# Sums of w_down's rows formed one pair later, one silu queued behind a copy, seven places for weights in the second half of down

## The chip, the cores and the metric

The kernel runs on one core of a Trainium2 chip. The metric is the device time of one execution in microseconds (us); lower is better. A core has a tensor engine (PE, with its weight loads shown as PEld), a vector engine (DVE), a scalar engine (ACT), GpSimd (POOL), and an engine that only issues transfers (SP). ACT and POOL can issue transfers too. Each engine works through its own list of instructions in order.

## The reference, cut to what matters

One layer of an encoder trunk on 512 tokens with 1024 channels, in float32. After the mixers and the cross-attention comes the gated MLP, and the change lies wholly in it:

```
hf = _rms_norm(x, norm_ffn_pre[l])
u = _dwconv_causal(hf @ w_up[l], ffn_dw[l]) + ffn_dw_b[l]     # 1024 -> 2 x 2816, causal conv of width 3
u_g, u_v = jnp.split(u, 2, axis=-1)
yff = (jax.nn.silu(u_g) * u_v) @ w_down[l]                    # 2816 -> 1024
x = x + _rms_norm(yff, norm_ffn_post[l])
```

## The kernel before, in words

**Precision.** Every float32 operand of a product is split into a high part (a cast on ACT: L202 for w_up, L1673 for w_down) and a low part (a subtraction on DVE: L203, L1674). A product is three matmuls: high by high, high by low, low by high (L245 is the line of all of them).

**The up projection (`up_jobs`).** The 2816 gated channels are 22 blocks of 128. Block j has a gate half (i = 0) and a value half (i = 1), each with a weight block of 1024 x 128. `plain(j, i)` computes a half in the direct way, into one PSUM bank; `done` then evacuates it on ACT (L1697, into the tile c), adds the two taps of the convolution on DVE (L627), and, after the value half, takes the silu of the gate half on ACT (L1700) and multiplies the two on DVE into `ns.quart` (L1702). Blocks 0 to 4, the even ones up to 18, and 20 and 21 are plain. The eight odd blocks 5 to 19 use `seven`, a scheme with seven products in place of eight: sums of weight quarters are formed on POOL (L1752 to L1756), sums of the tokens were formed once (`token_sums`, L1663 and L1665, on POOL, then split by `token_split`, L1669 and L1670), and the job runs in five bodies a to e. `body_a` makes a product into the bank `z.r2`, copies it to SBUF on ACT (L1778), and makes a second product into `z.r1`; `body_b` then accumulates into `z.r2` (L1783), so it must wait until the copy has read it. Between the bodies of odd block j lie the two halves of the plain block j − 1.

**Sums of w_down's rows (`Sums`, `ns.sums`).** The down projection uses seven products too, and its weight sums depend on nothing but w_down. The rows are taken in 11 pairs of 128-row blocks. For each pair, `load` brings two tiles of 512 KB from w_down, `add` forms four sums in place (L575 to L578, on POOL in this stage), and `store` writes the two tiles to a buffer in DRAM. Pairs 0 to 3 (`EARLY` is 4) are done much earlier, between other work. Pairs 4 to 10 are done in the up projection; their tiles `wp` use the two places dw0 and dw1, and their loads and stores are issued by ACT. Pair 4's load is issued in the first jobs of the up projection, its sums on POOL beside the token sums; then, at each odd block, one pair is stored, the next loaded, and its sums formed at the block's end. `sums_step` ties each to an instruction of `done` on the same engine.

**The down projection (`down_jobs`).** Two halves (phases), each over the 11 pairs of rows, each pair in two jobs, so 22 + 22 weight tiles ("raws"). The transfers (L594, by SP) bring them into four places dw0 to dw3, in turn; `weights` for tile n asks for tiles up to n + 2. The first phase makes four of the seven products in eight PSUM banks, `middle` evacuates them, and the second phase makes the other three. Its last four pairs are held back and multiplied bank by bank in `ends`, followed by the norm and the output.

**What sets the order.** Instructions are traced in program order, but a scheduler reorders them at build time by a simulated time line: each engine gets, among the instructions ready in that simulation, the one that stands first in the program. On the chip the lists then run in that fixed order. `tc.issue_after(x)` ties what it encloses behind instruction x on the same engine's list, without a wait for x to finish. Tiles with the same tag share a place, and a new tile waits until the last reader of the old one is done. In this program the tag `tokh` holds the high parts of the token sums during the up projection, and then (`late_places`, `down_places`) the sums of activations of pairs 4 to 10 (`pairs`) during the first half of down.

Of the kernel before, what the change touches and what calls it, by code (L numbers as in the profile page):

```python
# [25 lines left out]
P = 128  # L26
# [60 lines left out]
def hybrid_layer(ctx: ExitStack, tc: tile.TileContext, a: dict, out: bass.AP):  # L87
# [1112 lines left out]
    def then(f):  # L1200

        return None, None, f
# [485 lines left out]
    def up_jobs():  # L1688
# [1 line left out]
        HALF = S // 2  # L1690
        first, second = slice(0, HALF), slice(HALF, S)

        def done(j, i, ps):
            if i == 0:
                st[j] = ns.fp.tile([P, 2, S], F32, tag="c", name="c", bufs=2)
            c, ch = st[j], i * NF + j
            st["first"] = A.activation(c[:, i], ps, AF.Identity, bias=pc("fb", ch), scale=pc("fdw2", ch)).ins  # L1697
            st["taps"] = taps(c[:, i], ps, lambda k: pc("fdw01", k * 44 + ch), 3).ins
            if i == 1:
                A.activation(c[:, 0], c[:, 0], AF.Silu)  # L1700
                x = ns.quart[j // 2][:, 2 * (j % 2):2 * (j % 2) + 2]
                V.tensor_tensor(x.rearrange("p a b -> p (a b)"), c[:, 0], c[:, 1], ALU.mult)  # L1702

        def block(j, i):
            return cols(w_up, i * DFF + j * P)
# [1 line left out]
        def sums_step(what, q, anchor):  # L1707
            if q < NF // 2:
                with tc.issue_after(st[anchor]):
                    getattr(ns.sums, what)(q)  # L1710

        def plain(j, i, then=None):
            def body(hi, lo):
                ps = bank()
                channel_major(ps, (hi, lo), ns.hf)
                done(j, i, ps)
                if then:
                    then()
            return *block(j, i), body

        for n in range(4):
            def body(hi, lo, n=n):
                j, i = divmod(n, 2)
                if n == 0:
                    bg.drain("n0")
                ps = bank(("mm", "sc")[n % 2])
                if n == 3:
                    channel_major(ps, (hi, lo), ns.hf, first, lambda: bg.drain("n1"))
                else:
                    (channel_major if n else by_pass)(ps, (hi, lo), ns.hf, first)  # L1730
                held.append((j, i, ps, (hi, lo)))
                if n == 3:
                    open_ffn()
                    ns.sums.tile, ns.sums.queue = lambda: dw_tile("wp", 2), A
                    ns.sums.load(EARLY)
                    token_sums()
                    for j, i, ps, w in held:
                        (channel_major if i or j else by_pass)(ps, w, ns.hf, second)
                        done(j, i, ps)
            yield *cols(w_up, n % 2 * DFF + n // 2 * P), body, V, same, HALF_SHIFT  # L1740

        def seven(j):

            z = SimpleNamespace()

            def load_a():
                z.g, z.v = [load_block(j, i) for i in range(2)]
                w = split_weights(z.g, [P, NK, P], shift=HALF_SHIFT)
                z.s = ns.fp.tile([P, D], F32, tag="z7", name="sums2")
                a11, a12, a21, a22 = (x[:, c] for x in (z.g, z.v) for c in (slice(0, S), slice(S, D)))  # L1750
                s1, s2 = z.s[:, :S], z.s[:, S:]
                G.tensor_tensor(s1, a21, a22, ALU.add)  # L1752
                G.tensor_tensor(s2, s1, a11, ALU.subtract)
                G.tensor_tensor(a21, a11, a21, ALU.subtract)
                z.t = ns.fp.tile([P, S], F32, tag="th", name="s4")
                G.tensor_tensor(z.t, a12, s2, ALU.subtract)  # L1756
                return w

            def load_block(j, i):
                raw = dw_tile("wq", 2, 2)  # L1760
                SP.dma_start(raw.rearrange("p (k c) -> p k c", k=NK), block(j, i)[0])
                return raw

            def product(ps, w, k0, x, start):
                for k in range(4):
                    mm3(ps, w[0][:, k0 + k], w[1][:, k0 + k], x[0](k), x[1](k), start and k == 0, k == 3, True)

            def part(k0, t):
                return [lambda k, h=h: h[:, k0 + k, (first, second)[t]] for h in ns.hf]

            def summed(i):
                return [lambda k, h=h: h[:, i, k] for h in ns.tok]

            def body_a(*w):
                z.r1, z.r2 = bank("sc"), bank("tr")
                z.m = ns.fp.tile([P, 2, HALF], F32, tag="mu", name="mu")
                product(z.r2[:, first], w, 0, part(0, 0), True)
                A.copy(z.m[:, 0], z.r2[:, first])  # L1778
                product(z.r1[:, first], w, 4, part(4, 0), True)
                V.tensor_tensor(z.r1[:, first], z.r1[:, first], z.m[:, 0], ALU.add)  # L1780

            def body_b(*w):
                product(z.r2[:, first], w, 4, summed(1), False)  # L1783
                A.copy(z.m[:, 1], z.r2[:, first])
                product(z.r1[:, second], w, 0, summed(0), True)
                A.copy(z.m[:, 0], z.r1[:, second])

            def body_c(*w):
                z.w = w
                product(z.r2[:, first], w, 0, summed(2), False)  # L1790
                V.tensor_tensor(z.r2[:, second], z.r2[:, first], z.m[:, 0], ALU.add)

            def body_d(*w):
                product(z.r1[:, second], w, 0, part(4, 1), False)
                V.tensor_tensor(z.r1[:, second], z.r1[:, second], z.m[:, 1], ALU.add)
                done(j, 0, z.r1)

            def end():
                product(z.r2[:, first], z.w, 4, summed(3), False)
                done(j, 1, z.r2)  # L1800

            return (load_a, body_a, (lambda: split_weights(z.s, [P, NK, P], shift=HALF_SHIFT), None, body_b),
                    (lambda: split_weights(z.v, [P, NK, P], shift=HALF_SHIFT), None, body_c),
                    (lambda: split_weights(z.t, [P, 4, P], shift=HALF_SHIFT), None, body_d), then(end))
# [4 lines left out]
        def early_places():  # L1809
            ns.pair_sums = []  # L1810
            down_places(f"qa{NF // 2 - 1}", 2)

        def splits(*which):
            return lambda: [token_split(i) for i in which]

        def add(q):
            if q < NF // 2:
                ns.sums.add(q, G)
# [2 lines left out]
        yield plain(2, 0, splits(1))  # L1821
        yield plain(2, 1, splits(0))
        yield plain(3, 0, splits(2))
        yield plain(3, 1, splits(3))
        yield then(lambda: (early_places(), add(EARLY)))

        for q, j in enumerate(pairs, EARLY):
            load_a, body_a, b, c, d, e = pairs[j]
            a = load_a, None, body_a
            tail = {}  # L1830

            def first_half(hi, lo, tail=tail):
                tail.update(ps=bank(), w=(hi, lo))
                for k in range(4):
                    mm3(tail["ps"], hi[:, k], lo[:, k], ns.hf[0][:, k], ns.hf[1][:, k], k == 0, False)

            def second_half(j, tail=tail):
                hi, lo = tail["w"]
                for k in range(4, NK):
                    mm3(tail["ps"], hi[:, k], lo[:, k], ns.hf[0][:, k], ns.hf[1][:, k], False, k == NK - 1)  # L1840
                done(j, 1, tail["ps"])

            yield a
            yield plain(j - 1, 0)
            yield then(lambda q=q: sums_step("store", q, "first"))
            yield b
            yield (*block(j - 1, 1), first_half)
            yield then(lambda q=q: sums_step("load", q + 1, "taps"))
            yield c
            if j in (9, 13):  # L1850
                yield then(sums_of((j - 9) // 4))
            if j == NF - 3:
                yield then(lambda: down_places("z7", 2))
            yield d
            yield then(lambda j=j, f=second_half: f(j - 1))
            if j == NF - 3:
                yield then(sums_of(2))
            yield e
            yield then(lambda q=q: add(q + 1))
# [11 lines left out]
    def down_jobs():  # L1871
# [4 lines left out]
        def load(n):  # L1876
            while len(raws) < min(n, 2 * len(order)):
                (phase, q), job = order[len(raws) // 2], len(raws) % 2
                raw = dw_tile("dw")
                load_parts(raw, ns.sums.parts(phase, job, q))  # L1880
                raws.append(raw)

# [30 lines left out]

        def weights(phase, q, job):
            n = 2 * (phase * pairs + q) + job
            load(n + 3)
            if n == 0:
                activations(0, 0)
            if job and n + 1 < 2 * len(order):
# [184 lines left out]
```

## Time and profile before

| | |
|---|---|
| median of 3 runs | 1042.18 us (1041.12 to 1042.36) |
| the profiled execution: time, span | 1040.78 us, 1039.0 us |
| granted PE clock, mean | 0.997 |
| busy: PE, DVE, ACT, POOL | 1024.6, 860.9, 533.5, 263.9 us |
| the up projection's token sums to its last block | about 696 to 925 us of the span |
| first and last load of down (L594) | 875.2, 1011.5 us |

A row of the time order reads: start in us, duration in us, engine, line, operation, output <- inputs, and in square brackets the idle time of the engine ahead of it with what ended it. SPq, ACTq and POOLq are the engines' sequencers, where transfers are issued. In a row of waits stand: the waiting instruction, what it waited for, us in total, how often, the longest.

### The profile page before, as it was taken

To read this page: it belongs to the slowest core of one execution; us is meant where nothing else is said; L and a number is where in the kernel's file an instruction comes from. 1 tells how busy PE (TensorE), PEld (TensorE's weight loads), DVE (VectorE), ACT (ScalarE), POOL (GpSimd) and SP (SyncE) were. 2 spreads that over 40 slices of the span, in tenths; PEclk is the share of its full clock that TensorE was granted. 3 is DMA by queue.
4 is the path that set the end of the run, shared out by engine and by line. 5 is a ranking of instruction groups with operands and counts; after the bars stand their busy time and mean duration, and the time that the engine had idled before them with its cause. 6 is when DMAs were issued, how large, how long until landed. Compare 5 with 4: busy or idle time off the path is not lost.

```text
span 1039.0 us, 15182 instructions
## 1 busy us (share of the span) xinstructions
PE 1024.6 (99%) x5477; PEld 883.9 (85%) x5477; DVE 860.9 (83%) x1323; ACT 533.5 (51%) x893; POOL 263.9 (25%) x270
## 2 busy tenths in 40 slices
PE   8999999999999999999999999999899999999996
PEld 7888888888888988888888889998799899888885
DVE  7999999787788667888687798778879897799786
ACT  5322222376565365766634566654455455466662
POOL 4001000100020214342000031149376556026102
PEclk9999999999999999999999999999999999999999
DMA  7954344844534245766458843153456566326662
GB/s 254 315 168 107 102 155 144 269 142 115 150 97 133 83 136 151 201 183 170 148 182 262 244 128 119 60 157 107 159 186 199 182 220 211 103 81 196 211 204 88
DMA packets 194128, 169.40 MB, mean 163 GB/s; under 512 B 25295, under 2 KB 165692, under 8 KB 194053
## 3 DMA queue, kind: packets, MB, share of 16 engines
q1 hardware_dynamic: 187315, 145.08, 46.9%
q10 hardware_dynamic: 4178, 14.82, 3.9%
q0 software_dynamic: 2560, 8.54, 2.7%
q8 instruction: 43, 0.70, 0.3%
q14 instruction: 32, 0.26, 0.1%
HBM read 142.18 MB, written 26.23 MB: 162 GB/s over the span
## 4 chain that ended last, share of the span: by engine, by line
PE 90%; DVE 5%; ACT 2%; issue 2%; DMA 1%; ACTq 0%; SPq 0%; POOL 0%; POOLq 0%; DVEq 0%
PE ps_mm L245 39%; PE ps_av L245 25%; PE ps_tr L245 14%; PE ps_sc L245 10%; PE ps_tr L251 1%; DVE wl L203 1%; DMA dw<-sums 1%; DMA e<-in_w_in 1%; DVE c L627 1%; PE ps_mm L463 1%; PE ps_av L463 1%; DVE tokl L1670 0%; ACT wh L202 0%; DVE qa L1702 0%; DVE n L1674 0%
## 5 line engine op out<-in xcount | busy, mean ns | idle before, releaser
L202 ACT CAST wh<-wr 128x1024 fp32r<-128x1024 f32 (+1 forms) x124 | 129.4, 1046 | 193.6 <-PE ps_mm L245 67.5
L203 DVE TENSOR_TENSOR wl<-wr,wh 128x1024 fp32r<-128x1024 f32 (+1 forms) x124 | 163.6, 1321 | 31.8 <-ACT wh L202 31.2
L245 PE MATMUL ps_mm<-hth,wh 128*128 128x512 f32 (+1 forms) x472 | 173.5, 376 | 0.1
L245 PE MATMUL ps_mm<-htl,wh 128*128 128x512 f32 (+1 forms) x472 | 173.5, 376 | 0.0
L245 PE MATMUL ps_mm<-hth,wl 128*128 128x512 f32 (+1 forms) x472 | 173.2, 375 | 0.0
L245 PEld LDWEIGHTS ps_mm<-hth,wl 128*128 128x128 f32 x472 | 87.0, 188 | 15.7
L245 PEld LDWEIGHTS ps_mm<-hth,wh 128*128 128x128 f32 x472 | 87.0, 188 | 15.6 <-ACT hth L164 0.3
L245 PEld LDWEIGHTS ps_mm<-htl,wh 128*128 128x128 f32 x472 | 87.0, 188 | 15.3
L245 PE MATMUL ps_av<-hth,wh 128*128 128x512 f32 (+1 forms) x264 | 97.9, 371 | 0.0
L245 PE MATMUL ps_av<-htl,wh 128*128 128x512 f32 (+1 forms) x264 | 97.9, 371 | 0.0
L245 PE MATMUL ps_av<-hth,wl 128*128 128x512 f32 (+1 forms) x264 | 97.6, 370 | 0.0
L700 DVE SCALAR_TENSOR_TENSOR y<-y,par,y 128x508 f32<-128x508 f32 (+29 forms) x120 | 82.4, 725 | 0.0
L245 PEld LDWEIGHTS ps_av<-htl,wh 128*128 128x128 f32 x264 | 49.7, 188 | 8.2
L245 PEld LDWEIGHTS ps_av<-hth,wl 128*128 128x128 f32 x264 | 49.8, 188 | 8.1
L245 PEld LDWEIGHTS ps_av<-hth,wh 128*128 128x128 f32 x264 | 49.8, 189 | 7.9
L1673 ACT CAST wh<-dw 128x1024 fp32r<-128x1024 f32 x32 | 33.7, 1052 | 21.8 <-PE ps_av L245 6.2
L1674 DVE TENSOR_TENSOR wl<-dw,wh 128x1024 fp32r<-128x1024 f32 x32 | 39.4, 1233 | 6.3 <-ACT wh L1673 6.2
L1910 POOL TENSOR_TENSOR qa<-qa 128x256 f32<-128x256 f32 x11 | 26.6, 2431 | 58.5 <-DVE wr L1674 34.5
L245 PE MATMUL ps_tr<-htl,wh 128*128 128x512 f32 (+1 forms) x112 | 40.6, 363 | 0.0
L245 PE MATMUL ps_tr<-hth,wh 128*128 128x512 f32 (+1 forms) x112 | 40.6, 363 | 0.0
L245 PE MATMUL ps_tr<-hth,wl 128*128 128x512 f32 (+1 forms) x112 | 40.4, 360 | 0.0
L1127 POOL TENSOR_SCALAR fbias<-ck,cq 128x128 f32<-128x128 f32 (+3 forms) x32 | 21.4, 673 | 66.9 <-DVE st L1133 61.8
(558 smaller groups left out, 2737.3 us busy)
## 6 DMA issues: line engine op xcount, KB each, us to landing
wr<-in_w_in SPq DMA_DIRECT2D x38, 512.0 KB
wr<-in_w_gate SPq DMA_DIRECT2D x32, 512.0 KB
wr<-in_w_up SPq DMA_DIRECT2D x28, 512.0 KB
dw<-sums SPq DMA_DIRECT2D x44, 256.0 KB
wr<-in_w_branch SPq DMA_DIRECT2D x16, 512.0 KB
wq<-in_w_up SPq DMA_DIRECT2D x16, 512.0 KB
wp<-in_w_down ACTq DMA_DIRECT2D x14, 512.0 KB
sums<-wp ACTq DMA_DIRECT2D x14, 512.0 KB
```

Source lines behind the costliest of these rows:

```text
L202: last_weights[:] = [order(A.copy(hi, raw[:, :n])).ins, low.tensor_tensor(lo, raw[:, :n], hi.bitcast(F32), ALU.subtract).ins]
L203: low.tensor_tensor(lo, raw[:, :n], hi.bitcast(F32), ALU.subtract).ins]
L245: steps_of[:] = [PE.matmul(ps, lhs, rhs, start=start, stop=stop, skip_group_check=again).ins]
L251: turns.append(PE.transpose(ps, x, ident[:n, :n]).ins)
L463: keep(PE.matmul(banks[c][:, :S // 2], w[p == 1][:, k, c * P:(c + 1) * P], ht[p == 2][:, i * 4 + k, :S // 2], start=(i, p, k) == (0, 0, 0) ...
L627: ins = V.scalar_tensor_tensor(dst[:, s:], src[:, :S - s], w(k), dst[:, s:], ALU.mult, ALU.add)
L700: ins = V.scalar_tensor_tensor(dst[:, s:], src[:, :S - s], pc("conv_dw", k * 4 + j), dst[:, s:], ALU.mult, ALU.add)
L1127: G.tensor_scalar(bias[:, :w], ck[j][:, :w], -1.0, cq[:, qt, head:head + 1], ALU.mult, ALU.add)
L1673: A.copy(hi, x)
L1674: return V.tensor_tensor(lo, x, hi.bitcast(F32), ALU.subtract).ins
L1910: G.tensor_tensor(z[:, 1], z[:, 2], z[:, 1], ALU.subtract)
```

## The change

Three edits, all in the MLP.

1. The sums of w_down's pairs 4 to 10 move one odd block later. The load of pair 4 is no longer issued in the first jobs of the up projection but during block 5, behind an instruction of `done`; its sums are formed at the end of block 5; the first store is in block 7, and the store of pair 10 in block 19, where there was none.
2. For block 3, `done` stops after the taps. Its silu and multiply (now `product_of`) are traced inside `body_a` of block 5, and on ACT the silu is tied behind that body's first copy (L1778).
3. In the second half of down, a tile of three weight places, `dw2`, is laid where `pairs` lay (tag `tokh`). Of each seven weight tiles the first three go there, the other four to dw0 to dw3, and the transfers are asked for six ahead instead of three, from the last job but one of the first half.

```
-        def done(j, i, ps):
+        def done(j, i, ps, ends=True):
...
-            if i == 1:
-                A.activation(c[:, 0], c[:, 0], AF.Silu)
-                x = ns.quart[j // 2][:, 2 * (j % 2):2 * (j % 2) + 2]
-                V.tensor_tensor(x.rearrange("p a b -> p (a b)"), c[:, 0], c[:, 1], ALU.mult)
+            if i == 1 and ends:
+                product_of(j)
+
+        def product_of(j):
+            c = st[j]
+            A.activation(c[:, 0], c[:, 0], AF.Silu)
+            x = ns.quart[j // 2][:, 2 * (j % 2):2 * (j % 2) + 2]
+            V.tensor_tensor(x.rearrange("p a b -> p (a b)"), c[:, 0], c[:, 1], ALU.mult)
...
                     ns.sums.tile, ns.sums.queue = lambda: dw_tile("wp", 2), A
-                    ns.sums.load(EARLY)
                     token_sums()
...
-                A.copy(z.m[:, 0], z.r2[:, first])
+                copied = A.copy(z.m[:, 0], z.r2[:, first]).ins
+                if j == 5:
+                    with tc.issue_after(copied):
+                        product_of(3)
...
-        yield plain(3, 1, splits(3))
-        yield then(lambda: (early_places(), add(EARLY)))
-
-        for q, j in enumerate(pairs, EARLY):
+        yield plain(3, 1, splits(3), False)
+        yield then(early_places)
+
+        for q, j in enumerate(pairs, EARLY - 1):
...
-            yield then(lambda q=q: sums_step("store", q, "first"))
+            if q >= EARLY:
+                yield then(lambda q=q: sums_step("store", q, "first"))
...
-            yield then(lambda q=q: sums_step("load", q + 1, "taps"))
+            yield then(lambda q=q: sums_step("load", q + 1, "first" if q < EARLY else "taps"))
...
-                raw = dw_tile("dw")
+                if phase and len(raws) == 2 * pairs:
+                    parts["more"] = ns.fp.tile([P, 3, D], F32, tag="tokh", name="dw2")
+                k = (len(raws) - 2 * pairs) % 7
+                raw = parts["more"][:, k] if phase and k < 3 else dw_tile("dw")
...
-            load(n + 3)
+            load(n + (3 if n < 2 * pairs - 2 else 6))
```

More of the change, by code (lines that the diff above doesn't have):

```diff
@@ L1710, in sums_step, with plain @@
                     getattr(ns.sums, what)(q)
-        def plain(j, i, then=None):
+        def plain(j, i, then=None, ends=True):
             def body(hi, lo):
@@ L1715, in body @@
                 channel_major(ps, (hi, lo), ns.hf)
-                done(j, i, ps)
+                done(j, i, ps, ends)
                 if then:
```

## The prediction

> **What bounds the kernel now.** First the page's line of busy times, then the waits of the tensor engine (PE) from 640 us to the end, where all edited code lies.
>
> ```profile
> PE 1024.6 (99%) x5477; PEld 883.9 (85%) x5477; DVE 860.9 (83%) x1323; ACT 533.5 (51%) x893; POOL 263.9 (25%) x270
> ```
>
> ```profile
> PE ps_tr L245 <- ACT mu L1778: 3.1, 1, 3.1
> PE ps_mm L245 <- ACT n L1673: 0.9, 1, 0.9
> PE ps_mm L245 <- DVE n L1674: 0.3, 1, 0.3
> ```
>
> PE sets the time. An edit that takes no matmul away (none here does) can give only idle PE time and slow PE time, and from 640 us on the rows leave three waits: one of 3.1 us near 744 us and two together 1.2 us near 1016 us. Next the time order around the first.
>
> ```profile
> 733.58 0.28 PE L245 MATMUL ps_tr<-hth,wl 128*128 128x256 f32 x1
> ...
> 740.35 0.39 PE L245 MATMUL ps_mm<-hth,wl 128*128 128x512 f32 x1
> 743.83 0.38 PE L245 MATMUL ps_tr<-tokh,wh 128*128 128x256 f32 x1 [3.08 <-ACT mu L1778]
> ```
>
> ```profile
> 733.01 0.78 ACT L1697 ACTIVATE c<-ps_mm,par 128x512 f32<-128x512 f32 x1
> 733.68 1.04 ACT L1669 CAST tokh<-qa 128x1024 fp32r<-128x1024 f32 x1
> 741.27 0.63 ACT L1700 ACTIVATE c<-c 128x512 f32<-128x512 f32 x1 [6.54 <-DVE c L627]
> ...
> 742.74 0.77 ACT L1697 ACTIVATE c<-ps_av,par 128x512 f32<-128x512 f32 x1
> 743.42 0.36 ACT L1778 COPY mu<-ps_tr 128x256 f32<-128x256 f32 x1
> ```
>
> The bank that the copy L1778 reads was filled by 733.86 (733.58 + 0.28). The scalar engine (ACT) ran the copy 9.6 us later. It had been idle 6.54 us in front of the silu of pair 3 (L1700), which waited for the vector engine (DVE), and the copy stood three places behind that silu. PE cannot start the product of L1783 into the bank before it is read.
>
> ```profile
> 717.40 2.77 DVE L203 TENSOR_TENSOR wl<-wr,wh 128x1024 fp32r<-128x1024 f32 x1
> ...
> 737.51 1.22 DVE L203 TENSOR_TENSOR wl<-sums,wh 128x1024 fp32r<-128x1024 f32 x1
> ...
> 740.43 0.74 DVE L627 SCALAR_TENSOR_TENSOR c<-ps_mm,par,c 128x511 f32<-128x511 f32 x1
> ```
>
> DVE reaches the tap that releases the silu only at 740.43 to 741.17. One split takes 2.77 us at 717 and 1.22 us at 737. What differs is GpSimd (POOL), which works without a pause up to 733 us:
>
> ```profile
> 711.47 1.31 POOL L575 TENSOR_TENSOR wp<-wp 128x512 f32<-128x512 f32 x1
> ...
> 719.04 2.28 POOL L576 TENSOR_TENSOR wp<-wp 128x512 f32<-128x512 f32 x1
> ...
> 726.32 2.28 POOL L577 TENSOR_TENSOR wp<-wp 128x512 f32<-128x512 f32 x1
> 728.55 2.41 POOL L1665 TENSOR_TENSOR qa<-qa 128x1024 f32<-128x1024 f32 x1
> 730.91 2.29 POOL L578 TENSOR_TENSOR wp<-wp 128x512 f32<-128x512 f32 x1
> ```
>
> Then the clock in stretches cut at the gap and, in a second answer of the same view, one later stage (columns: length, then busy time of PE, PEld, DVE, ACT, POOL, granted clock, DMA share, GB/s):
>
> ```profile
> 740.70:743.80 3.10, 0.04 (x1) 0.00 (x0) 1.41 (x2) 2.53 (x5) 0.00 (x0) 1.00 0.46 189
> 743.80:748.00 4.20, 4.17 (x25) 4.18 (x26) 4.20 (x8) 2.41 (x5) 0.00 (x0) 0.68 0.72 236
> 748.00:749.00 1.00, 1.00 (x5) 0.80 (x5) 0.96 (x3) 1.00 (x2) 0.00 (x0) 0.65 0.61 175
> ```
>
> ```profile
> 880.00:900.00 20.00, 20.00 (x125) 17.99 (x124) 13.98 (x19) 10.10 (x15) 0.05 (x1) 1.00 0.41 118
> ```
>
> Right behind the gap the granted clock is 0.68 and 0.65 for about 5 us. So the gap costs more than itself: 4.17 x (1 − 0.68) + 1.00 x (1 − 0.65) = 1.33 + 0.35 = 1.7 us. Last, from the chain of waits, what PE takes at full clock for a run of matmuls 256 wide (0.12 us each) and 512 wide (0.23 us each):
>
> ```profile
> 871.27 1.42 PE ps_tr L245 x12
> ...
> 979.84 1.36 PE ps_sc L245 x6
> ```
>
> **The change, part by part.**
>
> (1) The product of pair 3 goes behind the copy of block 5. Two instructions move, the silu (0.63 us) and one multiply; none is added. The copy is then free to run once ACT has done L1697 of 733.01 and L1669 of 733.68 (ends 734.72); with the other L1697 (0.77) ahead of it, it ends near 734.72 + 0.77 + 0.36 = 735.9. PE asks for it at 740.7. The 3.08 us wait goes, with a cover of 4.8 us, and with it, I take it, the slow clock: 3.1 + 1.7 = 4.8 us.
>
> What is late next? Behind the silu stands the cast of the weights for block 4's second half (in the row left out, between L1700 and L1697). If nothing else changed, the silu would run at 741.27, that cast would end near 742.9 and its low part on DVE near 744.1 (1.22 us more), whereas PE, after two products of 12 matmuls of 0.12 us, would ask at 740.7 + 2.8 = 743.5. That is a remainder of 0.6 us, bounded by 0 and 0.6, unless DVE comes earlier, which part 2 does.
>
> (2) The sums start one pair later. Removed at 711 to 733: four POOL instructions, 1.31 + 2.28 + 2.28 + 2.29 = 8.16 us, and two loads of 512 KB on ACT's queue ahead of them. The token sum of 728.55 then ends near 731.0 − 5.9 = 725.1, and a DVE split meets POOL for 8.16 us less. By the two split rows DVE gets back at most 8.16 x (1 − 1.22/2.77) = 4.6 us, and nothing if its queue there was held by other inputs. I take 2.5 us, since the taps, which read PSUM, took 0.74 us in this stretch. On the sum it is worth only the 0.6 us above, already counted.
>
> The first load now goes out behind block 4's L1697, with no transfer ahead of it on its places; its POOL sums have until the next pair's POOL work is done. The pairs between keep their pattern with the number one lower. What is new lies at the other end, in the stage of block 19: four POOL sums and two stores.
>
> ```profile
> 871.46 0.33 ACTq L582 DMA_DIRECT2D sums<-wp  x1
> ...
> 893.17 0.78 ACT L1697 ACTIVATE c<-ps_mm,par 128x512 f32<-128x512 f32 x1
> ```
>
> ```profile
> 875.18 0.34 SPq L594 DMA_DIRECT2D dw<-in_w_down  x1
> ...
> 882.11 2.18 SPq L185 DMA_DIRECT2D wr<-in_w_up  x2
> ...
> 897.88 6.68 SPq L185 DMA_DIRECT2D wr<-in_w_up  x2
> ```
>
> The sums cost DVE at most the same 4.6 us there. From 880 to 900 us DVE is idle 20 − 13.98 = 6.0 us, which hides it. The last stores move from 871.46 to behind the L1697 at 893.17. Before, the first load of down into those places came 875.18 − 871.46 = 3.7 us behind the first store. Now it is due near 897, past the first two weight loads of the up projection (882.11) and beside the last two (897.88). On SP's queue, which is in order, those could be held a microsecond; they serve blocks 20 and 21, which are asked for only at the end of the up projection. I cost this at nothing; without that cover it is 1 us.
>
> (3) Seven places in the second half of down. No instruction is added; 10 of 22 loads get another address and all are issued six ahead instead of three. The place (the old pair sums) falls free when the last activation of the first half is split, about when the first such load could go anyway.
>
> ```profile
> 1011.48 0.32 SPq L594 DMA_DIRECT2D dw<-sums  x1
> ```
>
> ```profile
> 1013.51 1.05 ACT L1673 CAST dw<-dw 128x1024 fp32r<-128x1024 f32 x1 [1.10 <-DMA dw<-in_w_down]
> 1014.91 1.14 ACT L1673 CAST n<-dw 128x512 fp32r<-128x512 f32 x2 [0.35 <-DMA dw<-sums]
> ```
>
> ```profile
> ACT n L1673 <- DMA dw<-sums: 6.2, 5, 2.0
> ```
>
> ```profile
> 1016.10 0.50 PE L245 MATMUL ps_mm<-n,htl 128*128 128x512 f32 x1 [0.91 <-ACT n L1673]
> 1016.91 0.73 PE L245 MATMUL ps_mm<-n,htl 128*128 128x512 f32 x2 [0.31 <-DVE n L1674]
> ```
>
> The last load goes out at 1011.48 because a place was not free, and lands for the casts at 1014.91, which release PE. Three loads earlier is 1.5 pairs of PE work, so this chain starts some microseconds sooner than the 1.2 us that PE lacks. Bounds 0 and 1.2 us; I take 1.2, as ACT's casts of this kind waited 6.2 us for transfers and for little else. No slow clock follows here.
>
> [...]
>
> The sum: 3.1 + 1.7 + 1.2 = 6.0 us off the profiled execution, span 1039.0 to 1033.0, time 1040.8 to 1034.8 (1.8 us lie around the span). The median of the runs, 1042.18, is 1.4 us above that execution, so it goes to **1036.2**.
>
> **The rivals.**
>
> A. The tail stays. The last chain is bound by DVE and ACT work itself, not by the load. For it: DVE has many splits there; against: ACT's 6.2 us of DMA waits. Gain 4.8: 1037.4.
>
> B. A remainder of the gap. The order on ACT and DVE is made at build time; only the silu is tied. If the copy is queued behind L1697 of block 4, which needs the matmul of 740.35, it ends about 740.75 + 0.77 + 0.36 = 741.9 and 1.2 us of wait stay; with a late low part 0.6 more. Even with the slow clock kept, the gain is 6.0 − 1.2 − 0.6 − 1.7 = 2.5: 1037.4 to 1039.7.
>
> C. POOL's new work in the stage of block 19 holds DVE 4.6 us where it cannot catch up, and PE waits for splits at the start of down. For it: the doubled split under POOL. Against: 6.0 us of idle DVE. Gain 1.4: 1040.8. [...]
>
> D. It does not do what it says: ACT is held elsewhere ahead of the copy until past 743 and the tail stays too: 1042.
>
> E. Slower. The three new places are slices of one tile. If a load into one slice waits for readers of the others, then for three of every seven weights the load (1014.91 − 1011.48 = 3.4 us) and the split (1.05 + 1.22 = 2.3 us) run one after the other, 17 us, where PE works for about 14 (3.5 pairs of 18 matmuls of 0.23 us): 3 us lost in each of three rounds, 9 − 4.8 = 4 us slower: 1046. It decides as soon as a load into a slice is held by a neighbour. Against it stand four slices of one tile in the mixer's output:
>
> ```profile
> 568.23 0.33 SPq L594 DMA_DIRECT2D wide<-in_w_out  x1
> ...
> 571.37 0.33 SPq L594 DMA_DIRECT2D wide<-in_w_out  x1
> ```
>
> ```profile
> 570.12 2.35 DVE L165 TENSOR_TENSOR wl<-wide,wh 128x1024 fp32r<-128x1024 f32 x2
> ```
>
> The load of 571.37 goes out while DVE still reads another slice of the tile, until 572.47.
>
> **How the numbers follow.** Forecast 0.60, A 0.10, B 0.10, C 0.04, D 0.10, E 0.06. About 0.2% (2.1 us) is what a measurement here tells from no change. Faster: forecast, A and most of B, 0.78; same: the rest of B, C and D, 0.16; slower: E, 0.06. The range takes in the forecast, A and B: down to 1034.2, because the runs before spread 1.2 us and DVE's relief may free a little more, and up to 1039.8, which leaves out D and E and most of C, about 0.2.
>
> **What would show it.** Right: no PE wait for ACT L1778 and a granted clock of 1.00 behind it; the copy of block 5 near 736 on ACT with the silu of pair 3 behind it; no L575 to L578 on POOL before 745, and seven of them up to about 885; the last down loads issued several microseconds before their casts, and no PE wait for L1673. Wrong: a new PE wait for DVE L203 near 743, for L202 or L203 behind 900, or casts in the second half that wait for a load into the new tile.

## The result, and the profile after

| | median us | lowest to highest | executions |
|---|---|---|---|
| before, beside it | 1041.65 | 1038.94 to 1042.36 | 4 |
| after | 1032.99 | 1032.79 to 1035.12 | 4 |

The ratio is 0.9926, with a 95% interval from 0.9904 to 0.9949: 7.7 us faster (1041.65 x 0.0074), about 5 to 10 us by the interval; the two medians lie 8.7 us apart. Forecast were 1036.2 us and a range from 1034.2 to 1039.8. The direction and the waits were right; the time lies 1.2 us under the low end.

The profiled execution of after took 1035.12 us, span 1033.3 us, the slowest of the four. Its line of busy times:

```profile
PE 1024.4 (99%) x5477; PEld 883.0 (85%) x5477; DVE 864.0 (84%) x1323; ACT 534.4 (52%) x893; POOL 263.5 (26%) x270
```

PE does the same work as before (1024.6 us). From 640 us to the end no row has a wait of PE. The next four rows are of three stretches: around the old gap, the stage of block 19, and around the old tail wait (length, then busy time of PE, PEld, DVE, ACT, POOL, granted clock, DMA share, GB/s).

```profile
735.00:741.00 6.00, 6.00 (x33) 5.12 (x32) 5.96 (x8) 3.94 (x7) 0.00 (x0) 1.00 0.19 57
741.00:750.00 9.00, 9.00 (x65) 8.40 (x64) 6.72 (x10) 3.92 (x7) 0.00 (x0) 1.00 0.72 233
880.00:900.00 20.00, 20.00 (x120) 17.75 (x119) 13.58 (x18) 8.35 (x14) 5.27 (x3) 1.00 0.66 205
1008.00:1012.00 4.00, 4.00 (x19) 3.34 (x18) 2.32 (x3) 0.77 (x2) 0.00 (x0) 1.00 0.00 0
```

PE is busy all of each stretch and the clock is 1.00 in all four; before, it was 0.68 and 0.65 behind the gap. In the stage of block 19 DVE still has 20 − 13.58 = 6.4 us of idle time, with 5.27 us of POOL's sums now in it.

The time order of after on ACT, DVE and POOL around the old gap:

```profile
737.30 0.36 ACT L1781 COPY mu<-ps_tr 128x256 f32<-128x256 f32 x1
739.73 0.63 ACT L1704 ACTIVATE c<-c 128x512 f32<-128x512 f32 x1 [2.06 <-DVE c L627]
```

```profile
727.29 1.21 DVE L203 TENSOR_TENSOR wl<-wq,wh 128x1024 fp32r<-128x1024 f32 x1
```

```profile
720.09 6.73 POOL L1665 TENSOR_TENSOR qa<-qa 128x1024 f32<-128x1024 f32 x2
```

The copy (L1778 before, L1781 now) runs 6 us earlier than before, and the silu (L1704 now) behind it. POOL is through at 726.8 us instead of 733.2, and the split after that takes 1.21 us. Around the old tail wait, on SP and PE:

```profile
999.56 0.33 SPq L594 DMA_DIRECT2D dw<-in_w_down  x1
```

```profile
1010.48 1.52 PE L245 MATMUL ps_mm<-n,htl 128*128 128x512 f32 x6
```

The last load goes out 12 us earlier than before (1011.48), of which 4 us are what this trace has gained up to there, and the six products that had two waits among them run without a pause.

**A measure for the runs below.** The first 700 us are the same code in all kernels, but the first L1697 of the up projection starts anywhere from 702.8 to 704.9 us in the traces, for instance in before and in after:

```profile
704.11 0.77 ACT L1697 ACTIVATE c<-ps_mm,par 128x512 f32<-128x512 f32 x1
```

```profile
704.92 0.77 ACT L1697 ACTIVATE c<-ps_mm,par 128x512 f32<-128x512 f32 x1
```

So I compare the rest, the span less this start: 1039.0 − 704.1 = 334.9 us before and 1033.3 − 704.9 = 328.4 after, 6.5 us less within two traces. It also accounts for most of what parts this execution of after, 1035.12 us, from the traced one of the run whole below, 1032.82 us: its first L1697 starts 2.05 us later than the 702.87 us there. Why that start moves is not shown.

### The profile page after: what moved, and what is told of

Read it like the earlier page. It is cut to its first block, busy times and chain, and to the rows that moved or that the text cites. A ratio compares the mean times of both kernels' runs of the same rounds, so it can differ in the third digit from the quotient of the medians.

```text
span 1033.3 us, 15189 instructions
## 1 busy us (share of the span) xinstructions
PE 1024.4 (99%) x5477; PEld 883.0 (85%) x5477; DVE 864.0 (84%) x1323; ACT 534.4 (52%) x893; POOL 263.5 (26%) x270
## 4 chain that ended last, share of the span: by engine, by line
PE 95%; DVE 2%; DMA 1%; ACT 1%; issue 1%; POOL 0%; POOLq 0%; DVEq 0%; SPq 0%; ACTq 0%
PE ps_mm L245 41%; PE ps_av L245 26%; PE ps_tr L245 15%; PE ps_sc L245 11%; PE ps_tr L251 1%; PE ps_mm L463 1%; PE ps_av L463 1%; DVE e L860 0%; DMA xs<-in_x 0%; DMA ptl<-turned 0%; DVE e L1133 0%; DVE ptl L879 0%; ACT wh L202 0%; ACT e L1139 0%; DVE qk L820 0%
```

## The experiments

| kernel | median us (executions) | ratio to before, 95% | rest us | PE waits after 640 us |
|---|---|---|---|---|
| before | 1040.26 (29), 1040.04 (30), 1039.55 (11) | | 334.9 | 3.1; 0.9 + 0.3 |
| whole | 1033.08 (6) | 0.9928 [0.9909, 0.9947] | 328.2 | none |
| p1_product | 1037.61 (12) | 0.9970 [0.9957, 0.9984] | 331.9 | 1.3; 1.3 + 0.3 |
| p2_sums | 1037.12 (12) | 0.9966 [0.9952, 0.9980] | 330.7 | 0.7; 0.8 + 0.3 |
| p3_seven | 1037.85 (12) | 0.9969 [0.9955, 0.9982] | 333.0 | 3.1 |
| p12 | 1035.31 (9) | 0.9961 [0.9946, 0.9977] | 330.3 | 1.2 + 0.3 |
| p2_load_early | 1040.65 (10) | 1.0006 [0.9993, 1.0019] | 337.3 | 3.1; 1.6 + 0.3 |
| p2_tied | 1036.06 (8) | 0.9970 [0.9959, 0.9981] | 331.8 | 0.4; 2.1 + 0.3 |
| s1_ask_six_four_places | 1040.60 (10) | 1.0003 [0.9989, 1.0018] | 334.9 | 3.0; 1.0 + 0.3 |
| s2_ask_three_seven_places | 1037.90 (10) | 0.9984 [0.9974, 0.9993] | 333.2 | 3.2 |
| g3_more_copies | 1037.57 (1) | | 332.5 | 1.5; 1.6 + 0.3 |
| g4_more_copies | 1037.69 (1) | | 332.8 | 2.3; 0.8 + 0.3 |
| p12_look1, 2, 3 | 1037.21, 1034.96, 1034.19 (1 each) | | 332.4, 330.0, 329.6 | 1.8 + 0.3; 0.9 + 0.3; 0.5 + 0.3 |

The three medians of before belong to three sets of runs: whole, p1, p2 and p3 were timed beside the first, p12, p2_load_early, s1 and s2 beside the second, p2_tied beside the third. g3 and g4 have a single execution of before beside them, 1037.30 us, so only their traces are used. "1.2 + 0.3" is the pair of waits in the tail.

### The change again

The kernel after, unaltered, for its own spread and a second trace.

> The changed kernel again, in more rounds, with a second profile. Theory S (the trace's waits, at their real price): from the first evacuation of the up projection (L1697, 704.1 us before) to the end it is 6.5 to 6.9 us shorter than before in the profile, as in the first profile (6.7), and what the times show beyond that is spread of the unchanged first 700 us: the ratio comes to 0.9936 with an interval that holds it, and the start of that L1697 lies 1 to 3 us earlier than the 704.9 us of the first profile of the changed kernel whenever its time is near 1033 us. Rival G (the change gives more than its waits): the stretch from that L1697 to the end is shorter by 8 us or more in the fast executions, and the first 700 us are alike within 0.5 us.

1033.08 us, six executions within 0.8 us (1032.80 to 1033.60). The rest is 334.9 − 328.2 = 6.7 us shorter, again without a wait of PE. The runs of before beside it spread over 7 us (1038.16 to 1045.14).

### One edit at a time

The first edit alone (its code here and below in part):

```
-                A.copy(z.m[:, 0], z.r2[:, first])
+                copied = A.copy(z.m[:, 0], z.r2[:, first]).ins
+                if j == 5:
+                    with tc.issue_after(copied):
+                        product_of(3)
```

> Only the product of pair 3 goes behind the copy; the sums and the four places stay as before. The prediction's step: the copy of block 5 ends near 736, the 3.1 us wait and the slow clock go (4.9 us at the trace's prices), and a remainder of 0 to 1.3 us of PE wait near 742 stays, because DVE, still slowed by POOL, adds z.m into the bank of the next product only near 743. So 3.6 to 4.9 us shorter, clock 1.00 behind it. Rival: the sums are what held it, and this alone leaves more than 2 us of wait and the slow clock: under 2 us gained.

It takes 3.0 us off the rest. The wait for the copy is gone, and another stands behind it (waits of PE in this kernel, then DVE's rows):

```profile
PE ps_sc L245 <- DVE ps_sc L1787: 1.3, 1, 1.3
```

```profile
740.01 0.74 DVE L627 SCALAR_TENSOR_TENSOR c<-ps_mm,par,c 128x511 f32<-128x511 f32 x1
740.67 1.22 DVE L203 TENSOR_TENSOR wl<-wr,wh 128x1024 fp32r<-128x1024 f32 x1
741.80 0.74 DVE L627 SCALAR_TENSOR_TENSOR c<-ps_av,par,c 128x510 f32<-128x510 f32 x1
742.46 0.42 DVE L1787 TENSOR_TENSOR ps_sc<-ps_sc,mu 128x256 f32<-128x256 f32 x1
```

DVE is as late as before (the tap of 740.01 comes 36.4 us behind the first L1697, that of 740.43 in before 36.3), and its sum into the bank `z.r1` stands at the end of what it is late with.

The second edit alone:

```
-                    ns.sums.load(EARLY)
...
-        yield then(lambda: (early_places(), add(EARLY)))
-        for q, j in enumerate(pairs, EARLY):
+        yield then(early_places)
+        for q, j in enumerate(pairs, EARLY - 1):
```

> Only the sums start one pair later; the silu of pair 3 stays ahead of the copy. By the prediction this is worth at most 0.6 us on PE. Rival O (the two edits overlap): without POOL's 8.2 us of sums DVE releases the silu some 2.5 us sooner, the copy ends about 2 us sooner, PE waits about 1 us instead of 3.1 us, and a wait that short leaves the clock at 1.00: 3 to 4 us gained by this alone.

It takes 4.2 us off the rest, more than the first edit and far more than the 0.6 us that the prediction gave it. The copy is still behind the silu. But the silu starts at 737.62 us, 702.84 us being where this trace's first L1697 starts; before, these were 741.27 and 704.11. So DVE releases it (741.27 − 704.11) − (737.62 − 702.84) = 2.4 us sooner. PE's wait for the copy shrinks to 0.7 us, and the clock behind it stays at 1.00. PE's rows at the wait:

```profile
739.07 0.39 PE L245 MATMUL ps_mm<-hth,wl 128*128 128x512 f32 x1
740.17 0.39 PE L245 MATMUL ps_tr<-tokh,wh 128*128 128x256 f32 x1 [0.71 <-ACT mu L1777]
```

Without a wait the second row would start 0.23 us behind the first. It starts 740.17 − 739.07 = 1.10 us behind it, so the wait shown as 0.71 us costs 0.87.

The third edit alone:

```
+                if phase and len(raws) == 2 * pairs:
+                    parts["more"] = ns.fp.tile([P, 3, D], F32, tag="tokh", name="dw2")
...
-            load(n + 3)
+            load(n + (3 if n < 2 * pairs - 2 else 6))
```

> Only the seven places and loads six ahead. Theory S: both PE waits near 1016 us go, 1.2 us by the rows, 1.8 us at their real price (a PE row's end lies 0.16 us behind the next possible start); the wait of 3.1 us near 744 and its slow clock stay. Rival: the last chain is bound by ACT and DVE, and at most 0.4 us is gained.

It takes 1.9 us off the rest. The tail waits are gone; the gap and the slow clock are as before.

The first two edits together, with four places in the second half of down:

> Product behind the copy and sums later, four places as before. Both theories of the gap (either edit removes most of it, neither all) say: no PE wait near 742, clock 1.00, 4.9 us shorter from the first L1697 to the end than before, with the two waits near 1016 us left. If instead the parts only add by chance, a PE wait of 0.5 us or more is left near 742.

The rest is 334.9 − 330.3 = 4.6 us shorter; the gap is closed, clock 1.00, and the tail keeps 1.2 + 0.3 us, 0.3 more than in the trace of before. The parts alone give 3.0 + 4.2 = 7.2 us, together 4.6: each of them by itself takes away, in its trace, the slow clock and most of the one wait, and these can be gained only once.

### GpSimd's work, or the loads that move with it

In the second edit two loads of 512 KB and four POOL sums move together. First the attempt to leave pair 4's load early:

```
-        yield then(lambda: (early_places(), add(EARLY)))
+        yield then(early_places)
...
+            if q >= EARLY:
+                yield then(lambda q=q: sums_step("load", q + 1, "taps"))
```

> As the sums alone one pair later, but pair 4's two loads stay where they were, at the start of the up projection; only its four POOL sums and its stores move. Theory P (POOL's work slows DVE): like the sums alone, about 4.1 us shorter from the first L1697 to the end, PE wait for L1777 of about 0.7 us. Rival L (the 1 MB of transfers at 699 us delays the weights): the wait is back near 3 us and the clock falls.

This did not separate them. The build-time scheduler, free to, left the sums L575 to L578 at 710 to 732 us, where they were. What it says: the later pairs' loads and stores moved by one block and the time did not change (1.0006), so these are not what helps. Its tail is taken up below.

Then the same with the sums tied:

```
+                st["t"] = G.tensor_tensor(z.t, a12, s2, ALU.subtract).ins
...
+        def add_tied():
+            with tc.issue_after(st["t"]):
+                add(EARLY)
```

> Pair 4's two loads stay in the first jobs of the up projection, as before; only its four sums on GpSimd are tied behind the next odd block's own sums, so they run past 750 us instead of 710 to 732. If GpSimd's work is what holds the vector engine's splits back, the split near 725 us takes about 1.2 us instead of 3.4, the copy runs near 739.8 and PE waits 0.7 us for it, as in the kernel with the whole second edit; the span up to 900 us falls by 4 us. If the two 512 KB loads were the cause, the splits stay at 2.2 to 3.4 us and the wait at about 3.1 us with the slow clock behind it. The 1.2 us tail wait stays by either.

POOL's rows and DVE's split in this trace:

```profile
717.70 6.71 POOL L1665 TENSOR_TENSOR qa<-qa 128x1024 f32<-128x1024 f32 x2
...
752.75 1.30 POOL L575 TENSOR_TENSOR wp<-wp 128x512 f32<-128x512 f32 x1
```

```profile
724.88 1.21 DVE L203 TENSOR_TENSOR wl<-wq,wh 128x1024 fp32r<-128x1024 f32 x1
```

and in p2_load_early the same split, beside POOL:

```profile
722.77 3.41 DVE L203 TENSOR_TENSOR wl<-wq,wh 128x1024 fp32r<-128x1024 f32 x1
```

With the loads early in both, only the place of POOL's four sums differs. The split takes 1.21 us instead of 3.41, PE's wait for the copy falls from 3.1 to 0.4 us, and the clock behind it is 1.00. In p2_load_early DVE has no idle time from 715 to 739 us, so it is late by its own long instructions, not by waiting for POOL's results. So it is GpSimd's work beside DVE, not the two loads.

### Seven places, or the earlier asking

Loads asked for six ahead, with four places:

```
-            load(n + 3)
+            load(n + (3 if n < 2 * pairs - 2 else 6))
```

> The second half of down asks for its weights six tiles ahead, in the four places of before. Theory S (the number of places binds, since every late load went out when a place came free): no gain, PE waits near 1016 us of about 1.2 us stay. Rival (the moment of asking binds): up to 1.8 us gained.

No change: 1.0003, the rest 334.9 us as before. The other half alone, seven places and three ahead:

> Seven places in the second half of down, asked for three ahead as before. Theory S: as with seven places and six ahead, 1.8 us shorter from the first L1697 to the end, no PE wait near 1016 us. Rival (the moment of asking binds): the loads go out only three tiles ahead and the waits of 1.2 us stay.

No tail wait, and the rest 1.7 us shorter, against 1.9 with both. So the number of places is what binds.

### How long a wait costs the clock

To the second edit alone three or four copies of the same bank are added ahead of the one that PE waits for:

```
+                for _ in range(3 if j == 5 else 0):
+                    A.copy(z.m[:, 1], z.r2[:, first])
```

> The sums alone one pair later, with three more copies of the same bank queued on ACT ahead of block 5's copy (their output is written over later; nothing else changes). They lengthen PE's wait there from 0.7 us by 3 x 0.25 to about 1.5 us. If a wait must be near 3 us to cost clock, the clock behind it stays 1.00 and the kernel is 0.8 us slower than with the sums alone, from the first L1697 to the end. If the clock follows the wait's length, it falls below 1.00 for some us.

> The same with four more copies, with a weight cast of 0.95 us between them in ACT's order: PE's wait becomes about 2.7 us. If a wait of nearly the 3.1 us of before costs clock as well, the clock falls to about 0.65 for 5 us and 1.6 us are lost beside the wait; if the limit lies nearer 3 us, the clock stays 1.00.

Waits of 1.55 and 2.34 us near 742, and the clock stays at 1.00 behind both; the row of the second:

```profile
742.00:745.00 3.00, 2.72 (x21) 2.52 (x22) 3.00 (x5) 1.80 (x4) 0.00 (x0) 1.00 1.03 361
```

Against that, p2_load_early's tail, where the waits were only 1.64 + 0.30 us:

```profile
1016.00:1019.00 3.00, 2.70 (x8) 2.02 (x8) 1.99 (x3) 0.00 (x0) 0.00 (x0) 0.65 0.00 0
1019.00:1022.00 3.00, 3.00 (x12) 2.40 (x11) 1.01 (x2) 0.72 (x2) 0.91 (x3) 0.78 0.00 0
```

Here the clock fell. The kernel p12, which keeps only the tail wait, had given times in two groups (1034.3 to 1035.6 and 1037.2 to 1038.4), so three more executions of it were traced:

> The kernel with edits 1 and 2 and four places again, for its trace: its times lay in two groups, 1034.3 to 1035.6 and 1037.2 to 1038.4. If what parts them is the clock behind the tail wait, an execution of the upper group shows a granted clock of 0.6 to 0.8 in the 5 us behind the 1.2 + 0.3 us wait near 1010 us, and loses 1.5 us or more there; one of the lower group shows 1.00. If they part elsewhere, the stretch from the first up-projection activation to the tail is the same length in both and the difference lies ahead of it or around the span.

> A second execution of the same: lower clock behind the tail wait if its time is 1037 us or above, none if it is 1034 to 1036 us, by the theory that the clock parts them; no such relation by the other.

> A third execution of the same, with the same two expectations.

The first came out at 1037.21 us, the others at 1034.96 and 1034.19. The mean granted clock of the nine earlier executions parts them in the same way: 0.997 in the three of the upper group, 0.998 or 0.999 in the six others. PE's rows of the first:

```profile
1008.29 0.84 PE L245 MATMUL ps_mm<-n,htl 128*128 128x512 f32 x3
1010.89 0.50 PE L245 MATMUL ps_mm<-n,htl 128*128 128x512 f32 x1 [1.76 <-ACT n L1673]
1011.70 0.73 PE L245 MATMUL ps_mm<-n,htl 128*128 128x512 f32 x2 [0.31 <-DVE n L1674]
1012.27 0.96 PE L245 MATMUL ps_mm<-n,a 128*128 128x512 f32 x3
...
1017.31 0.39 PE L245 MATMUL ps_sc<-wh,hth 128*128 128x512 f32 x1
```

and its clock, with the same stretch of the second below it:

```profile
1012.00:1015.00 3.00, 3.00 (x10) 2.35 (x9) 2.28 (x3) 0.72 (x2) 0.14 (x1) 0.65 0.00 0
1015.00:1018.00 3.00, 3.00 (x11) 2.38 (x11) 0.49 (x1) 0.00 (x0) 0.77 (x3) 0.79 0.02 5
```

```profile
1010.24 0.50 PE L245 MATMUL ps_mm<-n,htl 128*128 128x512 f32 x1 [0.91 <-ACT n L1673]
...
1011.62 0.85 PE L245 MATMUL ps_mm<-n,a 128*128 128x512 f32 x3
...
1015.04 0.39 PE L245 MATMUL ps_sc<-wh,hth 128*128 128x512 f32 x1
```

The same 15 matmuls take 1017.31 − 1012.27 = 5.0 us in the one and 1015.04 − 1011.62 = 3.4 us in the other: 1.6 us of slow clock. From the first L1697 to the row before the tail wait the two agree within 0.01 us (1008.29 − 702.96 and 1008.50 − 703.17), so all of the 2.4 us between their rests comes from the tail: a longer wait (1.76 instead of 0.91 us) and the slow clock behind it.

## Why the prediction was right, and where it was wrong

**Right: the mechanism of all three edits.** The copy runs ahead of the silu; in p1 it starts at 735.82 us, near the time forecast. POOL's sums leave the stretch before 733; DVE gains 2.4 us there (taken: 2.5). PE has no wait and the clock is 1.00. That the 2.5 came so near is in part luck, as it was taken from bounds of 0 and 4.6 without being worked out. Part (1) and (2) together were to give 4.8 us and gave 4.6 in the traces (4.9 without the 0.3 us by which p12's tail wait is longer) and 1040.04 − 1035.31 = 4.7 in the medians. The slow clock was put at 1.7 us; the same matmuls up to 749 us, laid beside those of after, lost 1.6. It went with the gap, as assumed: in p1, p2_sums, p12 and whole, where at most 1.3 us of wait is left there, the clock is 1.00 from 740 to 752 us.

**Right: what was costed at nothing in block 19.** PE has no wait there, and the seventh L575 starts at 877.4 us. The first of the last stores (ACT's queue), the load of down behind it and the two weight loads of the up projection (SP's queue), in after:

```profile
889.05 0.33 ACTq L582 DMA_DIRECT2D sums<-wp  x1
```

```profile
891.99 0.33 SPq L594 DMA_DIRECT2D dw<-in_w_down  x1
...
894.11 6.58 SPq L185 DMA_DIRECT2D wr<-in_w_up  x2
```

The weight loads go out 3.8 us earlier than before (897.88), as PE's work does in this stretch, so nothing is held. Rival C did not happen. Nor did A, B and D: their waits are not there; nor E: with the third edit alone the rest falls.

**Wrong, the step that failed: "The median of the runs, 1042.18, is 1.4 us above that execution, so it goes to 1036.2".** The last step laid the 6.0 us on the median of three runs, 1042.18 us. In 29, 30 and 11 runs the median of the same kernel is 1040.26, 1040.04 and 1039.55 us, with a spread of 7 us in the first set. So the base was some 2 us too high, and the profiled execution (1040.78) was the better base. From 1040.2 the same sum would have given 1034.2. This is the larger part of the 3.2 us by which the forecast missed: 1042.18 − 1040.26 = 1.9. Why those three lay high is not shown, as no clock or trace of them is on record. The low end failed with it: "because the runs before spread 1.2 us" took three runs for the spread.

**Wrong in size: the tail, "bounds 0 and 1.2 us", "No slow clock follows here".** Four executions of p12, which lacks only the third edit, have rests of 329.6, 330.0, 330.3 and 332.4 us, and the whole change 328.2: the third edit is worth 1.4 to 4.2 us there. Made alone it took 1.9 us off the rest and 1040.26 − 1037.85 = 2.4 us off the medians, about twice the 1.2 us of the sum: these 1.2 us more are the rest of the 3.2. Two things were left out. These waits cost more than their rows show: the two waits in p12_look2 are 0.91 + 0.30 us, but PE's next rows lie 1.6 us late (the third matmul of 1008.50 starts at 1008.95, so without waits the row of 1011.05 would have come at 1009.41). And in some executions the clock does fall there, for 1.6 us more, shown in p12_look1 and p2_load_early.

With these the sum comes out: 4.7 us for the first two edits (p12) and 2.4 for the third (p3_seven) are 7.1 us, against 1040.26 − 1033.08 = 7.2 measured. The forecast had 6.0.

**Wrong, without weight for the whole: the parts of the gap.** The remainder of the first edit was put at 0 to 0.6 us, for a late cast and low part; p1 shows 1.3 us for DVE's sum L1787. The second edit was "worth only the 0.6 us". It is worth 330.3 to 331.9, 1.6 us, once the first is made, and 4.2 us by itself. The prediction followed the copy on ACT and did not look at what else stood in DVE's late queue.

**Open.** The clock's fall behind the tail wait is shown in two executions of kernels that keep that wait, not in one of before itself, whose only trace has 1.00 there. Before's spread goes with the clock all the same: of its 70 executions in the table, the 17 with a mean granted clock of 0.998 or 0.999 have a median of 1038.5 us, the 27 with 0.996 or 0.997 one of 1039.9, and the 26 with 0.994 or 0.995 one of 1041.6. Where the clock fell in these was not traced. A further part of the spread lies in the first 700 us, where the first L1697 starts up to 2 us apart from trace to trace for a cause that is not shown.

## What to carry to other kernels

A forecast stands on the time of before, and three runs of a kernel with waits on its way can have their median 2 us off: lay the gain on the profiled execution, whose steps have been followed, and widen the range by what the waits can vary. A wait of PE cost more here than its row: the one of 0.71 us in p2_sums delayed the next matmul by 0.87 us, and the two of p12_look1 had 1.6 us of slow clock behind them besides. Taking away the last of these waits also made the time steadier (nine of ten executions of after within 0.8 us, beside 29 of before within 7). When two edits work on one gap, price each with the other made and with it not made.

## What the runs showed of the hardware

**In these traces no fixed length of wait decides on the clock.** It fell, to 0.59 to 0.84 in the parts of the next 5 to 6 us, behind the gaps of 3.0 to 3.2 us in all five traces that have one (before, p3, s1, s2, p2_load_early). It fell, to 0.65 and then 0.78 or 0.79, behind 1.76 + 0.31 us (p12_look1) and 1.64 + 0.30 us (p2_load_early), but not behind 1.62 + 0.30 us (g3's tail), 2.34 us (g4) or 2.08 + 0.30 us (the tail of p2_tied):

```profile
1011.68 0.50 PE L245 MATMUL ps_mm<-n,htl 128*128 128x512 f32 x1 [2.08 <-ACT n L1673]
```

```profile
1013.00:1015.00 2.00, 2.00 (x10) 1.59 (x10) 1.69 (x3) 0.31 (x1) 0.00 (x0) 1.00 0.00 0
```

**What goes with the falls in these traces is the idle time within one stretch of 3.41 us.** Cut where the clock changes, p2_load_early shows two equal stretches at a granted clock of 0.50 (columns: length, PE's busy time, granted clock, DMA share, GB/s):

```profile
740.41:743.82 3.41, 1.25 (x10) 1.00 0.00 0
743.82:747.23 3.41, 3.41 (x17) 0.50 0.60 178
747.23:750.65 3.42, 3.42 (x20) 1.00 0.43 129
1013.48:1016.89 3.41, 1.46 (x6) 1.00 0.03 9
1016.89:1020.30 3.41, 3.41 (x10) 0.50 0.00 0
```

Each lasts 3.41 us, and the second starts 1016.89 − 743.82 = 273.07 us behind the first, 80.0 times 3.413. The slow stretch of before has the same length, and from its end to the fall at the end of that trace it is 1035.42 − 748.70 = 286.72 us, 84.0 times 3.413:

```profile
741.87:745.28 3.41, 1.45 (x12) 1.00 0.76 309
745.28:748.70 3.42, 3.42 (x16) 0.50 0.64 179
1032.00:1035.42 3.42, 0.08 (x1) 1.00 0.38 149
1035.42:1038.83 3.41, 0.00 (x0) 0.50 0.43 158
```

Cut back from that fall in steps of 3.413 us, before has 303 of them. The two in which PE was idle for 3.41 − 1.45 = 1.96 and 3.42 − 0.08 = 3.34 us are followed by a clock of 0.50; the other 301, with at most 1.5 us of idle PE, by 1.00. In after, cut back in the same way from its only fall, at 1030.94 us, one of 302 steps has 3.41 us and is followed by 0.50; the others have at most 1.2 us.

Ahead of the two slow stretches of p2_load_early PE was idle for 3.41 − 1.25 = 2.16 and 3.41 − 1.46 = 1.95 us of the step. In g3 nearly the same tail waits fall across the edge of two steps, with 0.45 and 1.47 us of idle time, and the clock stays at 1.00:

```profile
1008.13:1011.54 3.41, 2.96 (x14) 1.00 0.42 135
1011.54:1014.95 3.41, 1.94 (x7) 1.00 0.00 0
1014.95:1018.36 3.41, 3.41 (x17) 1.00 0.02 5
```

Closest to each other are p12_look1, with 1.73 us of idle time and a clock of 0.50 in the next step, and g4, with 1.63 us and 1.00:

```profile
1009.46:1012.87 3.41, 1.68 (x6) 1.00 0.00 0
1012.87:1016.28 3.41, 3.41 (x10) 0.50 0.00 0
```

```profile
740.65:744.07 3.42, 1.79 (x13) 1.00 0.76 247
744.07:747.48 3.41, 3.41 (x22) 1.00 1.01 356
```

So the 1.76 + 0.31 us of p12_look1 had a slow stretch behind them and the longer wait of g4, 2.34 us, of which 1.63 lie in the step shown, had none. What sets where the steps lie, and whether this holds beyond these traces, is not shown.

A fall cost 3.41 x 0.5 = 1.7 us by the clock (before, p2_load_early, p12_look1) and 1.6 us by the matmuls laid side by side (p12_look1 beside p12_look2).
